# Moving the last wait and the semaphore clear from GpSimd to the sync engine

## The chip, the cores and the metric

The kernel runs on one core of a Trainium2 chip. The metric is device time in microseconds (us), smaller is better. The kernel before takes 83.76 us (median of the first three runs, 83.73 to 83.87). Engines are named as in the profile: PE is TensorE, DVE VectorE, ACT ScalarE, POOL GpSimd, SP the sync engine.

## The reference

Cross entropy with label smoothing, over 256 rows of 32,000 classes in float32. Cut to what matters:

```python
log_probs = logits - np.max(logits, axis=-1, keepdims=True)
log_probs = log_probs - np.log(np.sum(np.exp(log_probs), axis=-1, keepdims=True))
smooth_targets = np.full((batch, num_classes), smoothing / num_classes)
for i, label in enumerate(labels):
    smooth_targets[i, label] = 1.0 - smoothing + smoothing / num_classes
return (-np.sum(smooth_targets * log_probs, axis=-1)).astype(np.float32)
```

The kernel must read 32.77 MB of logits once and return 256 numbers.

## The kernel before

SP loads the logits in pieces, ACT takes exponentials and sums them, DVE sums the logits, POOL fetches the label's logit and finishes the first of the two rows that each partition holds. PE turns columns into rows, and the last DVE instruction writes the result, which SP stores:

```python
    nc.vector.scalar_tensor_tensor(
        out=res[:, :, r : r + 1], in0=lin_row[:], scalar=-c_small,
        in1=lse_t[:], op0=ALU.mult, op1=ALU.add,
    )
    nc.sync.dma_start(
        out=out.rearrange("(g i) -> g i", g=1), in_=res[:].rearrange("g p r -> g (p r)")
    )
```

The framework closes a kernel with waits on SP for all that is in flight, a barrier of the five engines, a clear of the kernel's semaphores on POOL, and a second barrier. This kernel has already rewritten that: the second barrier is dropped, and the wait for the store stands behind the first barrier instead of ahead of it. The function that does so edits the finished instruction list:

```python
def _end_behind_one_barrier(nc) -> None:
    body, end = nc.m.functions[0].blocks[1:]
    # ... `landed` is the store's semaphore, `closing` the closing instructions
    waits = list(first.sync_info.on_wait)
    (store_wait,) = [w for w in waits if w.id == landed.id]
    closing[0] = replace(first, sync_info=mybir.SyncInfo(
        on_wait=[w for w in waits if w.id != landed.id], ...))
    clear = next(i for i, ins in enumerate(closing) if ins.opcode == "ISA")
    before = closing[clear - 1]          # a POOL drain, just ahead of the clear
    closing[clear - 1] = replace(
        before, sync_info=mybir.SyncInfo(on_wait=[store_wait], on_update=[])
    )
    end.instructions = closing[: clear + 1]
```

In the barrier, PE, ACT, DVE and SP each raise a "gather" semaphore and wait for a "release" semaphore; POOL waits for four gathers and then releases all four.

The softmax here doesn't subtract the row's maximum and nothing guards it: scores larger than these inputs give would overflow.

## Time and profile before

| before | us | from |
|---|---|---|
| measured time, profiled execution | 83.85 | run |
| span, first to last instruction of the kernel | 81.864 | trace |
| store issued by SP | 80.443 | trace |
| POOL's release of the barrier ends | 81.367 | trace |
| store landed (last increment of its semaphore) | 81.575 | trace |
| clear on POOL ends | 81.864 | trace |

Two sources have to be read together. The page and its views cover the kernel's own instructions, to a tenth or a hundredth of a microsecond. The trace also has a record of every change of every semaphore in nanoseconds, and that record goes on behind the kernel's last instruction. The prediction shows the lines of the views and uses both sources. In the views a q behind an engine's name stands for its sequencer.

### The profile page before, as it was taken

What the parts mean: (1) busy time and instruction counts of PE and PEld (TensorE: products, weight loads), DVE (VectorE), ACT (ScalarE), POOL (GpSimd) and SP (SyncE); (2) the same over time, 40 slices, a digit from 0 to 9 for tenths busy, and PEclk for the clock granted to TensorE, in tenths of its full rate; (3) what the DMA queues carried; (4) which work ended last, traced back from release to release, by engine and by line L of the source; (5) the groups of instructions that cost most, each with busy time, mean ns of one, the idle gap of its engine ahead of it and who ended that gap; (6) DMA issues with size and microseconds to landing.
All of it is one profiled execution on the core that took longest, in us unless ns stands there. A gap on an engine that the chain in (4) does not pass through costs nothing.

```text
span 81.9 us, 220 instructions
## 1 busy us (share of the span) xinstructions
PE 7.1 (9%) x21; PEld 5.0 (6%) x21; DVE 37.0 (45%) x37; ACT 57.8 (71%) x31; POOL 10.2 (12%) x19
## 2 busy tenths in 40 slices
PE   0000000000000000000000000000100000499511
PEld 0000000000000000000000000000000000488300
DVE  0000001990000799400199802990196839466772
ACT  5000001999200899994199999999999999999990
POOL 3200640040100000000000002991000000000000
PEclk9999999999999999999999999999999999999999
DMA  6999999999998888998799699999999999999900
GB/s 140 390 446 400 461 556 390 390 390 439 585 512 385 360 360 383 653 405 360 302 503 520 285 536 388 413 400 409 432 432 432 438 410 429 418 418 408 410 24 1
DMA packets 2258, 32.77 MB, mean 400 GB/s; under 512 B 337, under 2 KB 338, under 8 KB 1106
## 3 DMA queue, kind: packets, MB, share of 16 engines
q1 hardware_dynamic: 2018, 30.71, 88.3%
q10 hardware_dynamic: 144, 2.06, 5.9%
q0 software_dynamic: 96, 0.00, 0.1%
HBM read 32.77 MB, written 0.00 MB: 400 GB/s over the span
## 4 chain that ended last, share of the span: by engine, by line
DMA 53%; ACT 44%; issue 1%; PE 0%; DVE 0%; ACTq 0%
DMA wide<-in_logits_dram 53%; ACT ja L249 24%; ACT jt L249 19%; PE lse_t L256 0%; DVE res L365 0%; ACT lse L360 0%; ACT lse L290 0%; ACTq L249 0%
## 5 line engine op out<-in xcount | busy, mean ns | idle before, releaser
L249 ACT ACTIVATE ja<-wide 128x8000 bf16<-128x8000 f32 (+4 forms) x5 | 40.2, 8033 | 21.0 <-DMA wide<-in_logits_dram 20.9
L234 DVE SCALAR_TENSOR_TENSOR jd<-wide 128x4000 f32<-128x4000 f32 (+11 forms) x12 | 34.5, 2876 | 39.0 <-DMA wide<-in_logits_dram 39.0
L249 ACT ACTIVATE jt<-wide 128x4608 bf16<-128x4608 f32 (+6 forms) x7 | 14.2, 2068 | 0.0
L351 PE MATMUL warm<-wide,ident 128*128 128x256 f32 x18 | 6.2, 519 | 11.7 <-DMA wide<-in_logits_dram 11.7
L351 PEld LDWEIGHTS warm<-wide,ident 128*128 128x128 f32 x18 | 4.8, 272 | 13.0 <-DMA wide<-in_logits_dram 12.0
L256 PE MATMUL loss_t<-ident,loss 128*1 128x128 f32 x1 | 0.4, 370 | 58.6 <-POOL loss L292 58.6
L281 POOL TENSOR_TENSOR lin<-acc,weighted 128x1 f32<-128x1 f32 x1 | 4.5, 4483 | 0.1
L256 PEld LDWEIGHTS loss_t<-ident,loss 128*1 128x1 f32 x1 | 0.1, 79 | 58.6 <-POOL loss L292 58.6
L276 POOL TENSOR_TENSOR acc<-sums 128x2 f32<-128x2 f32 x1 | 0.2, 192 | 16.3 <-ACT ja L249 16.3
L167 POOL DMA_INDIRECT gat<-in_logits_dram,flat_idx x2 | 2.0, 994 | 0.7 <-POOL ident masks.py:199 0.4
L295 DVE COPY res<-loss_t 1x128 f32<-1x128 f32 x1 | 0.3, 280 | 3.7 <-PE loss_t L256 3.7
L134 ACT ACT_TABLE_LOAD x1 | 1.3, 1283 | 0.9 <-PEq L392 0.9
L276 POOL TENSOR_TENSOR acc<-acc,sums 128x2 f32<-128x2 f32 x1 | 0.2, 193 | 12.6 <-ACT ja L249 12.6
L193 POOL TENSOR_SCALAR weighted<-gat 128x1 f32<-128x1 f32 x1 | 0.9, 935 | 6.3 <-DMA gat<-in_logits_dram,flat_idx 6.3
L249 ACT ACTIVATE jt<-tail 128x704 bf16<-128x704 f32 (+1 forms) x2 | 1.5, 762 | 0.0
L249 ACT ACTIVATION_READ_ACCUMULATOR jt<-wide 128x1 f32 x7 | 1.2, 171 | 0.0
L234 DVE SCALAR_TENSOR_TENSOR jd<-tail 128x352 f32<-128x352 f32 (+1 forms) x2 | 1.0, 510 | 0.0
L234 DVE DVE_READ_ACCUMULATOR jd<-wide 128x1 f32 x12 | 1.0, 81 | 0.0
L147 POOL DMA_DIRECT2D lab<-in_labels_dram x1 | 0.8, 766 | 1.0 <-POOLq L392 1.0
L249 ACT ACTIVATION_READ_ACCUMULATOR ja<-wide 128x1 f32 x5 | 0.9, 172 | 0.0
L159 POOL TENSOR_TENSOR flat_idx<-rowoff,lab 128x2 int32<-128x2 int32 x1 | 0.2, 194 | 5.4 <-DMA lab<-in_labels_dram 5.4
L193 POOL TENSOR_SCALAR xsum<-gat 128x1 f32<-128x1 f32 x1 | 0.2, 207 | 2.8 <-DMA gat<-in_logits_dram,flat_idx 2.8
(24 smaller groups left out, 4.7 us busy)
## 6 DMA issues: line engine op xcount, KB each, us to landing
wide<-in_logits_dram SPq DMA_DIRECT2D x1, 6240.0 KB, 26.0
wide<-in_logits_dram SPq DMA_DIRECT2D x1, 5760.0 KB, 39.2
wide<-in_logits_dram SPq DMA_DIRECT2D x1, 4288.0 KB, 29.6
wide<-in_logits_dram SPq DMA_DIRECT2D x1, 3200.0 KB, 20.4
wide<-in_logits_dram SPq DMA_DIRECT2D x1, 2304.0 KB, 25.5
wide<-in_logits_dram ACTq DMA_DIRECT2D x1, 2016.0 KB, 13.8
wide<-in_logits_dram SPq DMA_DIRECT2D x1, 1984.0 KB, 11.5
wide<-in_logits_dram SPq DMA_DIRECT2D x1, 1696.0 KB
```

The source lines that it names most:

```text
L134: nc.scalar.add_instruction(mybir.InstLoadActFuncSet(name=nc.get_next_instruction_name(), act_func_set_id=tbl, ins=[], outs=[],))
L147: nc.gpsimd.dma_start(out=lab[:], in_=labels.bitcast(I32).rearrange("(p f) -> p f", p=P))
L159: nc.gpsimd.tensor_tensor(out=flat_idx[:], in0=rowoff[:], in1=lab[:].rearrange("p (r two) -> p r two", two=2)[:, :, 0:1], op=ALU.add,)
L167: nc.gpsimd.indirect_dma_start(out=gat[:, r : r + 1], out_offset=None, in_=logits[:], in_offset=bass.IndirectOffsetOnAxis(ap=flat_idx[:, r ...
L193: nc.gpsimd.tensor_scalar(out=weighted[r], in0=gat[:, r : r + 1], scalar1=label_weight, scalar2=None, op0=ALU.mult,)
L234: return nc.vector.scalar_tensor_tensor(out=jd[:, :h], in0=xt[:, :h], scalar=1.0, in1=xt[:, h:w], op0=ALU.mult, op1=ALU.add, accum_out=out,)
L249: return nc.scalar.activation(out=ja[:, :w], in_=xt[:, :w], func=AF.Exp, accum_out=out)
L256: nc.tensor.transpose(out=row[:], in_=column, identity=ident[:])
L276: nc.gpsimd.tensor_tensor(out=acc[:], in0=total, in1=sums[:, :, t : t + 1], op=ALU.add)
L281: nc.gpsimd.tensor_tensor(out=lin[:], in0=total[:, 0, :], in1=weighted[0], op=ALU.add)
L295: nc.vector.tensor_copy(out=res[:, :, 0:1], in_=loss_t[:])
L351: nc.tensor.matmul(warm[:], lhsT=ident[:], rhs=xt[:, i * WARM_COLS : (i + 1) * WARM_COLS], start=True, stop=True,)
```

## The change

The intent: POOL's drain is slow, so let SP wait for the store and clear the semaphores. The core of the diff (the checks around it, which move or are added, are left out):

```diff
     closing[clear - 1] = replace(
-        before, sync_info=mybir.SyncInfo(on_wait=[store_wait], on_update=[])
-    )
...
+        before,
+        engine=sync,
+        sync_info=mybir.SyncInfo(on_wait=[store_wait], on_update=[]),
+    )
+    closing[clear] = replace(closing[clear], engine=sync)
     end.instructions = closing[: clear + 1]
```

Two instructions change their engine. No other one changes, nor does the order on any engine ahead of them.

## The prediction

> **What bounds the kernel now.** I read the page first, for its span and its chain, and then the end of the chain piece by piece. The page and the chain of work give:
>
> ```profile
> span 81.9 us, 220 instructions
> PE 7.1 (9%) x21; PEld 5.0 (6%) x21; DVE 37.0 (45%) x37; ACT 57.8 (71%) x31; POOL 10.2 (12%) x19
> DMA 53%; ACT 44%; issue 1%; PE 0%; DVE 0%; ACTq 0%
> ...
> 78.80 0.70 ACT jt L249 x2
> 79.49 0.02 issue
> 79.52 0.27 ACT lse L360
> 79.79 0.04 issue
> 79.83 0.28 PE lse_t L256
> 80.11 0.02 issue
> 80.14 0.28 DVE res L365
> ```
>
> The columns of the last seven lines are start, length and what ran. Loads of the logits and exponentials on ScalarE are 97% of the chain, and the last counted work, the DVE instruction that writes the result, ends at 80.14 + 0.28 = 80.42 us. The change edits none of this. The span ends at 81.86 (81.864 unrounded), so 1.45 us lie behind the last compute, and only there can the change act directly. The timeline and the view of the closing line (it counts sequencer instructions, which the busy figures leave out) show what fills them:
>
> ```profile
> 80.44 0.32 SPq L373 DMA_DIRECT2D out_dram<-res  x1
> ...
> L406 SPq EVENT_SEMAPHORE  x7: 17/28/28, 80.8 to 81.4; - x7
> L406 POOLq DRAIN  x2: 97/326/555, 58.3 to 81.6; - x2
> L406 SPq DRAIN  x2: 7/7/7, 81.2 to 81.2; - x2
> L406 POOLq EVENT_SEMAPHORE  x2: 17/17/17, 81.3 to 81.3; - x2
> ...
> L406 POOLq EVENT_SEMAPHORE_RANGE_CLEAR  x1: 139/139/139, 81.7 to 81.7; - x1
> ```
>
> The three numbers after a count are the least, median and longest duration in ns; then come the first and last start. Of the two POOL drains the one at 81.6 takes 97 ns; the one at 58.3 takes 555 ns and lies inside POOL's earlier work. So: SP issues the store, goes through six waits and a drain, joins the barrier; POOL gathers and releases it; POOL alone then waits for the store, drains and clears 20 semaphores.
>
> The trace's records have these starts to the nanosecond. The store goes out from 80.443 to 80.766. POOL's release of the barrier ends at 81.367; SP, ACT, DVE and PE are through it by 81.408, 81.412, 81.423 and 81.454. The store's semaphore gets its last increment at 81.575. POOL's drain starts at 81.599, its clear at 81.725, and the clear ends at 81.864: that is the end of the span. Behind the barrier both POOL and SP would wait, so the landing of the store, not the barrier, sets the tail: it comes 0.17 us after SP is free.
>
> The measured time, 83.76 us (83.85 for the profiled execution), is 2.0 us more than the span. The records of semaphore changes go on behind the span: semaphore 2, which the kernel never touches, is changed nine times from 81.695 to 82.675, all other semaphores are reset between 82.578 and 83.240, and semaphore 2 is changed nine times again, to 83.970. That is work of the runtime, and of about the size of the 2.0 us.
>
> **What the Trainium skill says.** (1) "Runtime: NRT & Kernel Launch", section "The launch sequence", tells of a barrier behind the kernel, a reset of 51 semaphores per engine, and a second barrier; and that the sync barrier runs as a serpentine over five engines, 8 hops of 44 ns. The trace agrees: nine changes make eight hops, and the unobstructed barrier just ahead of the kernel takes 0.371 us from -0.375 to -0.004. Its hops are 35, 38, 44 and 23 ns out, 112, 38, 35 and 46 back. (2) "Perfetto Trace Analysis", section "Sequencer-only Instruction (DRAIN, etc)", says that such a record starts when its semaphores are satisfied, so a wait is not in its length. Here too: POOL was free at 81.367, but its drain is recorded as 97 ns from 81.599, 24 ns behind the store's last increment. (3) "DMA: Bandwidth & Descriptors" puts most of a DMA's fixed cost, about 2.0 us, in the receipt of the write. The store here takes 1.13 us from its issue's start to the last increment, less, but also far more than moving 1 KB. No engine that waits for it makes it land sooner.
>
> **The change, part by part.** The same drain with the same wait and the same 20-semaphore clear go to SP. Nothing is removed from the program, no barrier and no wait.
>
> Part one, inside the span. Store landed: 81.575. A DMA issue on SP was released 17 ns after the DVE's increment (80.426 to 80.443), so SP's drain should start about 81.595. SP's two drains take 7 ns, POOL's 97, so it ends at 81.60. SP's sequencer instructions follow each other 31 to 40 ns after the end of the one before (80.834 to 80.870, 80.898 to 80.932, ...), where POOL took 29. The clear then starts at 81.64. It takes 139 ns on POOL; SP has no such record here, but both take 17 ns for a barrier step, so I keep 139. End: 81.78, against 81.864. The span should fall by about 0.085 us, which is 0.1%.
>
> Part two, behind the span. The first runtime barrier has its changes at 81.695, 81.729, 82.390, 82.435, 82.458, then 82.555 to 82.675. The gap of 661 ns before the third is not there ahead of the kernel (38 ns). All others are as in the free one, so exactly one engine held it up, the third. If engines go in the order PE, ACT, POOL, DVE, SP, as I take it, that is POOL: its increment comes 526 ns after its clear ends, whereas PE's, the first, comes 241 ns after PE's last instruction. So POOL is not only late by its wait, drain and clear; it also seems slower to get from the kernel to the runtime's barrier. With the change POOL is free at 81.367 and can be in the barrier at 81.367 + 0.526 = 81.893; DVE follows at 81.94 and SP could at 81.96. But SP is now held: 81.78 plus its own way to the barrier. If that is like PE's 0.241, its increment comes at 82.02; if like POOL's 0.526, at 82.31. Before, SP's stood at 82.458. So the turn of the serpentine, and with it all that follows rigidly, comes 0.15 to 0.44 us sooner. I take the middle, 0.30 us: 83.76 - 0.30 = 83.46 us.
>
> **The rivals.** First: the measured time doesn't contain that barrier, or something else behind it holds; then only part one counts, 83.76 - 0.085 = 83.67. For it: I infer what the time covers from a sum alone. Against it: the 2.0 us above the span match the records behind it.
> Second: the clear is slow on SP, or SP is slower than POOL to leave the kernel. With 0.1 us more for the clear and a way of 0.53 the turn is at 82.41, and 0.05 us remain: 83.71. Nothing in the profile speaks for it; SP's 7 ns drains speak against it. A loss would need SP to take over 0.68 us from the end of its clear.
> Third: the landing is hidden behind the barrier, so that who waits doesn't matter. The trace speaks against that, by 0.17 us on SP; and even then POOL's longer drain would go.
> Fourth: the loads move. SP issues them, but its added instructions come behind the last one, so a change of the 80.4 us before the store would be noise; the three runs of before spread over 0.14 us.
>
> **Range and chances.** The best case of part two (0.44) with 0.07 us of noise gives 83.25; at the other end part one alone, with an unlucky noise of 0.05, gives 83.72. A verdict of 2% needs 1.68 us. All that lies between the last compute and the end of the span is 1.45 us, and the change touches 0.29 us of it, plus at most some tenths behind. Hence 0.98 for within 2%, and 0.01 for each side, for a surprise in the runtime's code.
>
> **What would show it.** In the changed kernel's closing line, the drain and the clear should stand at SP, 7 and about 139 ns, POOL's last event being the barrier step, and the span should be near 81.8, if the chain up to 80.42 is the same. In the semaphore records the third change of semaphore 2 should come about 0.5 us sooner, and the long gap should stand before the fifth (SP's), not the third. The prediction is wrong if SP's clear is much longer than 139 ns, if the gap stays with the third engine, or if the time falls by no more than the span.

## The result, and the profile after

The changed kernel took 83.30 us (median of 6 runs, 83.21 to 83.37), the kernel before beside it 83.80 us (83.73 to 84.07). The ratio is 0.9934, with a 95% interval of 0.9919 to 0.9949. A ratio here is the mean time of one kernel's fast runs over that of the other's of the same rounds, so it is not quite the ratio of the medians. The gain is real, and below 2%.

First the page of the changed kernel, its span and its chain, and the end of that chain (start, length, what ran):

```profile
span 81.6 us, 220 instructions
...
DMA 53%; ACT 44%; issue 1%; PE 0%; DVE 0%; ACTq 0%
...
79.43 0.27 ACT lse L364
79.70 0.04 issue
79.75 0.28 PE lse_t L260
80.03 0.02 issue
80.05 0.28 DVE res L369
```

The chain is the same to the percent, and its last three instructions have the same lengths. The last one starts at 80.05 instead of 80.14. Nothing in the change reaches that far up; the runs below show that this start moves from execution to execution by more than that.

Then the store's issue and the closing line of the changed kernel (least, median and longest duration in ns, first and last start in us):

```profile
80.36 0.32 SPq L377 DMA_DIRECT2D out_dram<-res  x1
...
L410 SPq EVENT_SEMAPHORE  x7: 17/28/28, 80.7 to 81.3; - x7
L410 SPq DRAIN  x3: 7/7/7, 81.1 to 81.5; - x3
L410 POOLq EVENT_SEMAPHORE  x2: 17/17/17, 81.2 to 81.3; - x2
L410 POOLq DRAIN  x1: 557/557/557, 58.2 to 58.2; - x1
...
L410 SPq EVENT_SEMAPHORE_RANGE_CLEAR  x1: 65/65/65, 81.6 to 81.6; - x1
```

SP has a third drain, at 81.5, and the clear. POOL's only drain left is the one at 58.2, and its last instruction is the barrier step that ends at 81.282. Note the clear: 65 ns on SP, where the same instruction took 139 ns on POOL. The view of the waits on SP's queue has a new row, which did not exist before:

```profile
SPq L410 <- DMA out_dram<-res: 0.2, 1, 0.2
```

SP waits 0.2 us for the store (total, times, longest). From landing to the end of the span it was 0.289 us before (81.575 to 81.864); it is 0.134 us now (81.489 to 81.623). So the span's tail is 0.155 us shorter. The other 0.09 us of the shorter span is the earlier store.

But 0.155 us is not 0.5 us. What decides lies behind the span. Here are the semaphore records of both profiled executions, in us behind the landing of the store:

| | before | after |
|---|---|---|
| kernel's last instruction ends | 0.289 | 0.134 |
| first change of semaphore 2 | 0.120 | 0.121 |
| second | 0.154 | 0.155 |
| third | 0.815 | 0.378 |
| fourth | 0.860 | 0.421 |
| fifth | 0.883 | 0.444 |
| ninth, end of the runtime's first barrier | 1.100 | 0.661 |
| last change, end of its second barrier | 2.395 | 1.956 |

Everything from the third change on comes 0.44 us sooner, as one block. Three things can be read from it. The third change is still held up: 223 ns behind the second, where a free barrier has 38. The fifth follows the fourth by 23 ns, as in a free barrier, so SP, which the prediction expected to be the late one, is not. And the measured time moves with all this: counted from the kernel's first instruction, the last change comes 83.970 - 83.85 = 0.120 us later than the reported time before, and 83.445 - 83.32 = 0.125 us later after. In all ten profiled executions that difference is 0.116 to 0.131 us.

### The profile page after: what moved, and what is told of

The parts are those of the page before. It is cut to its first block, busy times and chain, and to the rows that moved or that the text cites. A ratio compares the mean times of both kernels' runs of the same rounds, so it can differ in the third digit from the quotient of the medians.

```text
span 81.6 us, 220 instructions
## 1 busy us (share of the span) xinstructions
PE 7.7 (9%) x21; PEld 5.5 (7%) x21; DVE 37.0 (45%) x37; ACT 57.8 (71%) x31; POOL 10.1 (12%) x19
## 4 chain that ended last, share of the span: by engine, by line
DMA 53%; ACT 44%; issue 1%; PE 0%; DVE 0%; ACTq 0%
DMA wide<-in_logits_dram 53%; ACT ja L253 24%; ACT jt L253 19%; PE lse_t L260 0%; DVE res L369 0%; ACT lse L364 0%; ACT lse L294 0%; ACTq L253 0%
## 5 line engine op out<-in xcount | busy, mean ns | idle before, releaser
L355 PE MATMUL warm<-wide,ident 128*128 128x256 f32 x18 | 6.8, 562 | 11.7 <-DMA wide<-in_logits_dram 11.7
```

Source lines behind the costliest of these rows:

```text
L355: nc.tensor.matmul(warm[:], lhsT=ident[:], rhs=xt[:, i * WARM_COLS : (i + 1) * WARM_COLS], start=True, stop=True,)
```

## The experiments

Eight runs were made, one of them the changed kernel again; all were correct. An engine's way is the time from its last instruction in the kernel to its own change of semaphore 2, and a hop is the time from one such change to the next. Theory P: the third engine of the runtime's barrier is POOL, and its own way, 0.585 us in the changed kernel, is what still holds the third change. Rival S: the third engine is SP, whose clear ends 0.244 us ahead of the third change, just as PE needs 0.241 us. Rival U: part of the 0.5 us is luck upstream. The first four runs were sent together, the last four later and to another chip; each group had its own runs of the kernel before beside it.

### after_again: the changed kernel again

No edit.

> The changed kernel once more, as a control with more rounds. Theory T (the gain lies wholly behind the landing of the store): ratio to before 0.993 to 0.996, that is 0.35 to 0.55 us less; in the profile 0.13 us from landing to the end of the span (before 0.29), and the third change of the runtime's semaphore about 0.38 us behind the landing (before 0.815). Rival U (part of the 0.5 us is luck upstream: the store went out 0.085 us sooner in the one profile): the ratio falls back to 0.996 or nearer to 1, and the store's issue comes at 80.44 again.

Measured: 83.32 us (83.28 to 83.55, 5 runs) against 83.74 us (83.64 to 83.87, 9 runs), ratio 0.9958 (0.9944 to 0.9971). The store was issued at 80.373, landed at 81.504, and every entry of the table above came out within 1 ns of the first profile. So the tail's 0.44 us is fixed, and the store did not go back to 80.44, as rival U had it. Rival U can still hold for a small part: between 80.27 and 80.67 us, the store's issue in the ten profiled executions has a spread of 0.40 us. That is enough for the median gains of 0.50 and 0.42 us to differ; that it made them differ is not shown, since executions without a profile do not tell when their store went out.

### pool_drain4: four more drains on POOL

```diff
+    extra = [
+        replace(before, name=f"I-90{i}", engine=pool, sync_info=None) for i in range(4)
+    ]
-    end.instructions = closing[: clear + 1]
+    end.instructions = closing[: clear - 1] + extra + closing[clear - 1 : clear + 1]
```

> The changed kernel with four more POOL drains, without a wait, behind POOL's release of the barrier. Theory P (POOL is the third engine of the runtime's barrier and its own way of 0.585 us still holds it): each drain with its gap took 0.126 us before, so the third change comes 0.5 us later than in the changed kernel, and the time goes back up by 0.5 us to about 83.8. Rival S (the third engine is SP, whose 0.244 us from its clear's end to the third change would then be like PE's 0.241): POOL's drains are hidden, the third change stays 0.24 us behind the clear's end, and the time stays at 83.3.

Measured: 83.74 us, ratio to before 1.0004 (0.9989 to 1.0020). The closing line of this kernel:

```profile
L413 POOLq DRAIN  x5: 78/83/555, 58.2 to 81.7; - x5
...
L413 SPq EVENT_SEMAPHORE_RANGE_CLEAR  x1: 65/65/65, 81.5 to 81.5; - x1
```

SP did all that it does in the changed kernel, at the same time behind the landing to 1 ns, and the whole gain is gone. The drains took 97, 83, 78 and 78 ns, from the start of the first to the end of the last 0.417 us rather than 0.50. A gap of 0.064 us stands ahead of them, and POOL's way behind them is about as much shorter, 0.519 us against 0.585. So the third change moved from 0.378 to 0.802 us behind the landing, by 0.42. POOL is the third engine, and these drains behind its release were paid in full. Rival S falls.

### sp_wait12: twelve more instructions on SP

```diff
+    (met,) = [ins for ins in closing[:1]]
+    extra = [
+        replace(
+            met,
+            name=f"I-9{i:02d}",
+            sync_info=mybir.SyncInfo(on_wait=waits[:1], on_update=[]),
+        )
+        for i in range(12)
+    ]
-    end.instructions = closing[: clear + 1]
+    end.instructions = closing[:clear] + extra + closing[clear : clear + 1]
```

> The changed kernel with twelve more waits on SP, all for a semaphore that is long met, between SP's drain and its clear: 12 x (17 + 36) ns = 0.64 us by the spacing seen before. Theory P: the third change stays about 0.585 us behind POOL's last barrier step, and the long gap moves to the fifth change, which then tells SP's own way from its clear's end; with a way of 0.24 us SP has 0.07 us to spare and the time rises by 0.57 us, with 0.1 us by 0.43. Rival S: the third change moves by the full 0.64 us, and so does the time.

They came out as drains with a met wait, 7 ns each and 55 ns apart:

```profile
L419 SPq DRAIN  x15: 7/7/7, 81.3 to 82.4; - x15
```

The clear ended 0.797 us behind the landing instead of 0.134, 0.663 us later. The third change did not move (0.377), and the long gap stood ahead of the fifth (0.903). From the clear's end to the fifth change it is 0.106 us: that is SP's own way into the runtime's barrier. So in the changed kernel SP could have made its change at 0.134 + 0.106 = 0.240 us, but the barrier reached it at 0.444: SP had 0.204 us to spare. The fifth change moved by 0.459 us, and 0.663 - 0.204 is 0.459. The time was 83.71 us (83.60 to 83.97), 0.39 us above the changed kernel; the profiled execution, 83.97, had a late store. The hop behind SP's change took 44 ns instead of 97, which gives 0.05 us back. The spare time says more: in the changed kernel neither the landing of the store nor SP's clear bounds the time. The 0.155 us that the span's tail lost was worth nothing by itself; SP could have cleared 0.204 us later for the same time.

### no_release: the engines leave without a release

Shortened, with comments added; `gather` is POOL's wait for the four reports.

```diff
-    end.instructions = closing[: clear + 1]
+    for ins in closing[: clear - 1]:
+        if ins.opcode == "EventSemaphore" and ins.sync_info.on_update:
+            continue                             # no gather on POOL, no releases
+        if ins.engine == sync and ins.sync_info.on_update:
+            ins = replace(gather, engine=sync)   # SP waits for the four reports
+        elif ins.engine == pool:
+            ins = replace(ins, ...)              # POOL reports like the others
+        kept.append(ins)
+    end.instructions = kept + closing[clear - 1 : clear + 1]
```

SP still clears only when all four have reported and the store has landed; nobody uses the cleared semaphores behind their report.

> A version that should beat both: PE, ACT, DVE and POOL only report that they are done and leave, without waiting for a release; SP gathers the four reports, waits for the store and clears. Theory P: POOL's way is then over long before, and the barrier waits for SP alone: clear's end plus SP's way. With a way of 0.24 us SP's change comes 0.37 us behind the landing, where the changed kernel has it 0.444 behind, so 0.07 us less, 83.23; with 0.1 us it would be 0.2 us less, 83.1. Rival S: nothing but SP counted already, so the third change stays 0.24 us behind the clear's end and the time stays within 0.03 us of the changed kernel.

Measured: 82.87 us (82.82 to 83.01), ratio to before 0.9904 (0.9889 to 0.9919). It beats both kernels. Its page and closing line:

```profile
span 81.5 us, 214 instructions
...
L432 POOLq DRAIN  x1: 555/555/555, 58.1 to 58.1; - x1
...
L432 SPq EVENT_SEMAPHORE_RANGE_CLEAR  x1: 65/65/65, 81.5 to 81.5; - x1
```

POOL is through at 58.7 us. The first four changes of semaphore 2 come at 80.217 to 80.487, ahead of the landing, and the fifth 0.240 us behind it, which is exactly what sp_wait12 made of SP. That gains 0.204 us on the changed kernel, the upper end of what was expected; the whole gain is 0.45 us of medians. The records show the rest: the barrier's way back is 0.054 us shorter (0.163 against 0.217, the 44 ns hop again), and from its end to the last change it takes 1.155 us instead of 1.295. The last part was not foreseen. It is one hop of the second barrier, from the third change to the fourth, 49 ns instead of 196.

### wait_ahead and wait_ahead_sp: the wait ahead of the barrier

wait_ahead leaves all on POOL and gives SP back the wait for the store, ahead of the barrier. wait_ahead_sp does the same and has the drain and the clear on SP.

In both:

```diff
-            on_wait=[w for w in waits if w.id != landed.id],
+            on_wait=waits,
```

In wait_ahead:

```diff
-        engine=sync,
-        sync_info=mybir.SyncInfo(on_wait=[store_wait], on_update=[]),
-    )
-    closing[clear] = replace(closing[clear], engine=sync)
+        engine=pool,
+        sync_info=None,
+    )
```

In wait_ahead_sp:

```diff
-        sync_info=mybir.SyncInfo(on_wait=[store_wait], on_update=[]),
+        sync_info=None,
```

> Nothing moved to SP: SP waits for the store ahead of the closing barrier, with the other waits, and POOL drains and clears behind the barrier. By the parts seen so far the barrier's release ends 0.27 us behind the landing (from SP's last wait to POOL's release it took 0.25 us before), then POOL's 0.026 + 0.097 + 0.029 + 0.139 and its way of 0.526 us: the third change 1.09 us behind the landing, where the kernel before has 0.815; time about 84.0. Rival (the runtime's barrier hides such things): 83.74 as before.

> The clear alone moved to SP, with the store still awaited ahead of the barrier: POOL's release at 0.27 us behind the landing plus its way of 0.585 us is 0.855 us, so 0.235 us less than wait_ahead and 0.04 us more than the kernel before: about 83.78. If instead the clear's move is what gains and the wait's place doesn't matter, it would come near the changed kernel, 83.32.

Measured: wait_ahead 84.20 us (84.01 to 84.38), ratio 1.0054 (1.0029 to 1.0078), third change 1.122 us behind the landing against 1.09 expected. wait_ahead_sp 83.91 us (83.67 to 84.12), ratio 1.0011 (0.9981 to 1.0041), so not told apart from before by time; its third change is at 0.851 against 0.855 expected. Both profiled executions had late stores (80.507 and 80.666), so the records are the better measure. They make a two by two of the third change behind the landing:

| us | POOL clears | SP clears |
|---|---|---|
| wait ahead of the barrier | 1.122 | 0.851 |
| wait behind it | 0.815 | 0.378 |

Taking drain and clear off POOL is worth 0.27 us where the wait stands ahead; where POOL also waited, it is worth 0.44.

### clear_PE: PE in the place of SP

```diff
-        engine=sync,
+        engine=mybir.EngineType.PE,
...
-    closing[clear] = replace(closing[clear], engine=sync)
+    closing[clear] = replace(closing[clear], engine=mybir.EngineType.PE)
```

> The changed kernel with PE in the place of SP: PE waits for the store behind the barrier and clears. Its way was 0.241 us, and it is the first of the runtime's barrier, so with 0.17 to 0.25 us for its drain, gap and clear the first change comes 0.41 to 0.49 us behind the landing and the third two hops (0.073) later, at 0.48 to 0.56 against 0.378 in the changed kernel: 0.10 to 0.18 us more, 83.42 to 83.50. If any engine but POOL were as good as SP, 83.32.

Measured: 83.47 us (83.41 to 83.50), ratio to before 0.9965 (0.9948 to 0.9981). The closing line:

```profile
L410 PEldq DRAIN  x2: 13/168/323, 79.7 to 81.5; - x2
...
L410 PEldq EVENT_SEMAPHORE_RANGE_CLEAR  x1: 185/185/185, 81.6 to 81.6; - x1
```

The clear takes 185 ns on PE, the third of three values for one instruction. The first change comes 0.487 us and the third 0.560 us behind the landing, 0.18 us later than with SP. It matters who does it, and not only that POOL doesn't.

### release_DVE: no release, but for DVE

The lines in which it differs from no_release, shortened, with comments added.

```diff
+            if ins.engine == mybir.EngineType.DVE:
+                kept.append(ins)                 # DVE waits for a release
+            elif ins.engine == pool and not ins.sync_info.on_wait:
+                kept.append(...)                 # SP gives it, one more drain
             continue
```

> The version without a release, but DVE alone waits for one from SP, ahead of the store's landing. In the runtime's second barrier DVE's change came 0.58 us behind the end of the reset there, against 0.72 us in the changed kernel. Theory D (it is DVE's early leaving that shortens this): the gap of about 0.15 us ahead of DVE's change in the second barrier is back, and the time is 0.14 us more than without any release, 83.0. Rival (it is due to something else): the time stays at 82.87 and the hop at 0.05 us. The first barrier should not change: the fifth change 0.24 us behind the landing.

Measured: 83.06 us (83.01 to 83.14), ratio to before 0.9916 (0.9900 to 0.9933). The fifth change is at 0.240 us, as in no_release; from the ninth to the last change it takes 1.298 us, as in all kernels with a release, and the hop to the fourth change of the second barrier is back at 198 ns. DVE was let go at 81.36 us instead of 80.29, by one more drain on SP well ahead of the landing, and that brought the 0.14 us back. So DVE's early leaving shortens its later stretch. Why it does is not recorded and stays open. The same run shows DVE's place in the first barrier: the fourth change moved from 80.487 to 81.556 us, each time 0.20 us behind DVE's last instruction.

All kernels in one table, in us from the records of the profiled executions; "landing to last" holds what the change can influence, free of the luck in the loads:

| kernel | landing to third | to fifth | fifth to ninth | ninth to last | landing to last | median time |
|---|---|---|---|---|---|---|
| before | 0.815 | 0.883 | 0.217 | 1.295 | 2.395 | 83.74 to 83.80 |
| changed | 0.378 | 0.444 | 0.217 | 1.295 | 1.956 | 83.30 |
| after_again | 0.378 | 0.444 | 0.217 | 1.296 | 1.957 | 83.32 |
| pool_drain4 | 0.802 | 0.869 | 0.216 | 1.296 | 2.381 | 83.74 |
| sp_wait12 | 0.377 | 0.903 | 0.164 | 1.297 | 2.364 | 83.71 |
| no_release | early | 0.240 | 0.163 | 1.155 | 1.558 | 82.87 |
| wait_ahead | 1.122 | 1.189 | 0.218 | 1.294 | 2.701 | 84.20 |
| wait_ahead_sp | 0.851 | 0.919 | 0.216 | 1.293 | 2.428 | 83.91 |
| clear_PE | 0.560 | 0.627 | 0.218 | 1.296 | 2.141 | 83.47 |
| release_DVE | early | 0.240 | 0.163 | 1.298 | 1.701 | 83.06 |

## Why the prediction was right or wrong

**Right for the span, wrong for the time: what bounds the tail.** The landing of the store, and not the closing barrier, sets the end of the span, before and after. The store took 1.13 us from issue to last increment in the kernel before and in the changed one, whoever waited. But the time of the changed kernel is set by the closing barrier: from its release, which ends 0.924 us behind the store's issue and 0.207 us ahead of the landing, POOL takes 0.585 us to the third change.

**Right in its mechanism, part one mis-sized.** SP's drain took 7 ns and started 17 ns behind the landing, much as worked out. The step "so I keep 139" failed: the clear took 65 ns on SP. The gap ahead of it took 45 ns, not the 31 to 40 that the prediction read off SP's instructions; it had left out the one gap behind a drain there, 48 ns (81.192 to 81.240). From the landing the tail was predicted at 81.78 - 81.575 = 0.205 us and measured at 0.134; the gain inside the span was 0.155 us rather than 0.085.

**Right: the barrier behind the span counts, and POOL was the late engine.** The order PE, ACT, POOL, DVE, SP, which the prediction only took, is shown for POOL by pool_drain4 (third), for SP by sp_wait12 (fifth), for PE by clear_PE (first) and for DVE by release_DVE (fourth). That leaves the second place to ACT, which no experiment delayed.

**Wrong: "But SP is now held".** This is the step that made the forecast 0.30 us instead of 0.44. Its term was SP's own way to the barrier, put between PE's 0.241 and POOL's 0.526 us. It measured 0.106 us in sp_wait12 and 0.107 in no_release, less than either. SP was ready 0.204 us before the barrier reached it, and the changed kernel is held by POOL once more: the prediction's own sign of error, "the gap stays with the third engine", came true. POOL's way was mis-sized too, on the other side: 0.585 us behind a barrier step, not the 0.526 it took behind the clear. With the measured terms, on the time scale of the kernel before, POOL's change is at 81.367 + 0.585 = 81.952 and the fifth, 66 ns on, at 82.018, against 82.458: 0.44 us, which is what the records show. By its parts: POOL no longer sits from 81.367 to 81.599 (0.232), no longer drains and clears to 81.864 (0.265), and loses 0.059 of that on its longer way.

**The range.** 83.30 us lies just inside it, near its fast edge. But the kernel before, run beside it, took 83.80 us and not 83.76: as a gain the range reaches 0.51 us (83.76 - 83.25), and the first comparison gave 0.50 by the medians and 0.55 by the ratio (0.0066 x 83.8), at and beyond its edge. The second gave 0.42. The best case that the prediction gave, 0.44, is the measured gain of the tail, but by luck: there it was SP's change at 81.78 + 0.241 = 82.02, which held nothing, and here POOL's and the two hops behind it, 81.952 + 0.066 = 82.018. Taking the middle of an interval whose ends were two other engines' values was the choice that went wrong; nothing in the profile spoke for the slow end on SP, whose drains were already seen to take 7 ns against 97.

**The rivals.** The first (the time doesn't contain the barrier) fell: the reported time follows the last change of semaphore 2 within 15 ns over ten executions. The second (a slow clear or way on SP) fell: both are the shortest measured. The third (the landing hidden behind the barrier) fell for the kernel's own barrier, as the prediction said: SP waits 0.17 us for the store behind it. Behind the span the prediction missed that it comes true: the landing, with SP's drain, clear and way, is hidden by 0.204 us behind POOL's way. The fourth, luck in the loads, may account for the difference between the two comparisons; it is not shown.

**What the prediction took from the skill on the store.** It is right that the 1.13 us are far more than the moving of 1 KB, one packet of 56 ns. That most of them are the receipt of the write, the trace does not bear out: the packet starts 0.741 us behind the issue, and the last increment comes 0.391 us behind that start. The argument does not rest on it.

**Open.** What POOL does in its 0.52 to 0.585 us between the kernel's last instruction and the runtime's barrier is not recorded.

## What to carry to other kernels

The end of the kernel's span is not the end of the measured time: ask which engine reaches the runtime's barrier last, and read that from the semaphore records. Give what must stand at the very end to the engine with the cheapest sequencer steps and the shortest way out, which here was SP, and let every other engine, POOL above all, leave as soon as its own work is reported rather than wait for a release. That last step, not part of the change studied, was worth as much again (82.87 against 83.32 us).

## What the Trainium skill lacked or had wrong

- "Runtime: NRT & Kernel Launch", section "The launch sequence": it has the serpentine and its sum (about 355 ns), which fits the 371 ns of the free barrier here. It lacks the order of the engines and the time that each needs from its last instruction in the kernel to its own change: 0.106 us for SP, 0.20 for DVE, 0.20 to 0.25 for PE, 0.52 to 0.585 for POOL. The hops are also not 44 ns each: 23 to 112 in the free barrier, and the one at the turn took 112, 97 or 44 ns by the run.
- The same section puts the reset at 51 semaphores per engine and about 1.5 us; here the recorded changes took 0.66 us in all (82.578 to 83.240), and its five blocks from 0.08 to 0.35 us each.
- No page that I found gives the cost of the range clear by engine. For the same 20 semaphores: 65 ns on SP, 139 on POOL, 185 on PE.
- "VectorE: DVE Perf Modes", section "The DRAIN you can't avoid", gives about 12 ns for the runtime's drains on all engines. For the kernel's own closing drains the engine matters: 7 ns on SP, 13 on PE, 78 to 97 on POOL with nothing left to wait for.
- "DMA: Bandwidth & Descriptors", section "Anatomy of one DMA — SWDGE (gpsimd) path": the fixed 2.0 us is a fit for GpSimd's path, and the page has no such fit for a DMA that SP issues. The 1 KB store on SP took 1.13 us here from issue to its last increment. The same section puts most of the fixed cost in the receipt of the write; of this store's 1.132 us, 0.741 had passed before its packet started, and 0.391 followed.
